# A hand-ordered decoder layer: ScalarE's weight split moved between join and taps, VectorE's adds a chunk later

## The chip, the core and the metric

The kernel runs on one core of one Trainium2 chip. The metric is the device time of one execution in microseconds; less is better. The engines are TensorE (PE, with PEld for its weight loads), VectorE (DVE), ScalarE (ACT), GpSimd (POOL) and SyncE (SP), which issues most DMAs. Each engine takes its instructions in the order in which the program issues them.

## The reference

One decoder layer in float32, for 256 tokens of width 2048:

```
h    = rms_norm(x, g1);  proj = h @ w_in            # q, k, v, p
a    = attention(norm(q), norm(k), v, rel_bias)     # 8 heads of 128, causal
m    = multiscale_pool(p, pool_w, pool_scale)
x    = x + concat(a, m) @ w_out
u    = rms_norm(x, g2) @ w_up                       # 2 * 5632 columns
y    = conv_b + sum_i conv_w[i] * u[t - 2 + i]      # causal, width 3, per column
gate, val = split(y)
x    = x + (silu(gate) * val) @ w_down
```

The last four lines, the gated feed-forward with the convolution between, are where the change lies.

## The kernel before

**Precision.** Each float32 operand of a product is split in a high part (rounded by a ScalarE copy to the matmul type) and a low part (VectorE: operand minus high part). A product is high x high + high x low + low x high. Weights arrive by DMA as raw tiles and are split on the fly: `high(c)` is the ScalarE copy (wh, L182), `low(c)` the VectorE subtraction (wl, L188).

**Rows, chunks and steps.** The weights lie in HBM as a list of rows (chunks) of 128 x 2048 numbers, in the order of use. A chunk of kind "feat" or "tok" has two steps, one of kind "sum" or "rest" a single one. The loop at the end of `layer` goes over the steps. At the first step of chunk r it issues `high(r+3)` on ScalarE, then `low(r+2)` on VectorE, then the weights' sums (`make`) that are set for r+2, then what the agenda holds for this step, then the list `deferred`, and then the matmuls. `later(2, f)` puts f in the agenda two steps after the first step of the current chunk, for feat chunks the start of the next chunk.

**Feed-forward in thirds.** The 22 groups of 256 gate and 256 value columns are done in thirds of 8, 8 and 6 groups. First come the up blocks of a third, for each group g a gate block and a value block, of two feat chunks each (called R0, R1 for the gate and R2, R3 for the value block here). Then comes the down stage of the third, in two halves, in which the pairs of `SEVEN` use a seven-product scheme in place of eight: it needs sums of weight quarters (`make`, VectorE L196 to L198, written to HBM from its raw tile and loaded again as a "sum" chunk) and sums of activation quarters (`left_sums`, L860 to L865). `BY_DVE` says at which groups of each third the weights' sums are made.

**After each up block** its post function runs, at the end of the block's second chunk:
- `conv_in`, the join: ScalarE copies one half of the PSUM result (fs, L545), VectorE adds the other half (L546) and multiplies with the row factor into u (L801).
- `conv`, the taps: six ScalarE instructions form the three products of the convolution from u (y, L811, and z, L813).
- `rest`, through `deferred` at the start of the next chunk: `taps`, two VectorE adds (L819; called the adds here), then Silu on ScalarE for a gate block (L832), or VectorE's product with the gate (L845) and ScalarE's high part of hid (L846) for a value block.
- `rest2`, a chunk after a value block's rest: hid's low part (L850) and, where the pair is one of seven products, `left_sums`, with ScalarE's high part (L864). Its low part (L865) waits in the list `pending` until the next gate block's post function.

**Buffers.** raw tiles: five; wh: four; wl: three; PSUM results of up blocks: two; the scratch tiles of fs and z: two together; u: one for gate and one for value blocks; the buffer of left sums (ls) is shared with the gate's y (tag y0).

Of the kernel before, what the change touches and what calls it, by code (L numbers as in the profile page):

```python
# [23 lines left out]
F32 = mybir.dt.float32  # L24
F32R = mybir.dt.float32r
AF = mybir.ActivationFunctionType
OP = mybir.AluOpType
AX = mybir.AxisListType

P = 128  # L30
D = 2048
S = 256
# [5 lines left out]
NF = DFF // P  # L38
# [17 lines left out]
STAGES = (0, 2, 4, 6)  # L56
EARLY = (72, 72, 80, 80)
BY_DMA = ((), (), ())
BY_DVE = ((2, 3, 4, 5, 6, 7), (0, 0.5, 1, 2, 3, 4, 5, 6, 6.5, 7), (0, 1, 2, 3, 4, 5))
SOFF, SPAD = 32, 64  # L60


# [6 lines left out]
def plan():  # L69

    rows = [(k, i) for i, k in enumerate(24 * ["tok"] + 25 * ["feat"])]
    makes, t = [(u, None) for u in EARLY], 0
    for (g0, g1), sevens, by_dma, by_dve in zip(THIRDS, SEVEN, BY_DMA, BY_DVE):
        c = rows[-1][1] + 1
        makes += [(2 * c + u, None) for u in by_dma] + [(None, len(rows) + int(4 * p) + 3) for p in by_dve]
        rows += [("feat", c + i) for i in range(4 * (g1 - g0))]
        c = rows[-1][1] + 1
        for i in range(2 * (g1 - g0)):
            if i % (g1 - g0) in sevens:
                rows.append(("sum", t))  # L80
                t += 1
            rows.append(("rest" if i % (g1 - g0) in sevens else "tok", c + i))
    assert len(makes) == t, (len(makes), t)
    return rows, makes
# [12 lines left out]
def layer(ctx: ExitStack, tc: tile.TileContext, xT, wts, mix, mix12, par, rel_d, ident_d, icnt_d, out):  # L97
    nc = tc.nc
# [15 lines left out]
    def small(name):  # L114
        return sm.tile([P, 512], F32, name=name, tag="small")
# [3 lines left out]
    def col(c):  # L119
        return pv[:, c:c + 1]  # L120
# [3 lines left out]
    rows, makes = plan()  # L124
# [6 lines left out]
    late, turn_of = {}, [0]  # L131
# [93 lines left out]
    def load_next():  # L225

        if order:
            c = order.pop(0)
            if not isinstance(c, tuple) and c < KT // 2:
                load_xT(2 * c, 2 * c + 2)  # L230
            load(c)
# [94 lines left out]
    ps = small("ps_start")  # L326
# [91 lines left out]
    rrow = keep.tile([P, S], F32, name="rrow", tag="rrow")  # L418
# [124 lines left out]
    def add_halves(dst, ps):  # L543

        nc.scalar.activation(dst, ps[:, :, S:], AF.Copy)  # L545
        nc.vector.tensor_tensor(dst, ps[:, :, :S], dst, op=OP.add)  # L546
# [52 lines left out]


    steps, hooks, pre, deferred = [], [], {}, []
    hold, splits, now, agenda, pending = set(), [], [0], {}, []
    where = []

    def later(n, f):
        agenda.setdefault(now[0] + n, []).append(f)
# [12 lines left out]
    def feat_block(act, ks, post, final=False):  # L619
        box, runs = {}, []  # L620
        for i, k0 in enumerate(ks):
            def run(u, i=i, k0=k0):
                if i == 0:
                    box["acc"] = None if final else acc("ps_feat")
                    box["ps"] = [small("ps_feat")[:, :S] if final else box["acc"][:, m, :] for m in range(2)]
                feat_half(u, act(), k0, box["ps"], i == 0, i == len(ks) - 1, feat_sum if final else feat_mm)
                if i == len(ks) - 1:
                    post(box["ps"] if final else box["acc"])
            runs.append([run])
        return runs  # L630
# [46 lines left out]
    for b in range(2):  # L677
# [6 lines left out]
        for j in range(4):  # L684
            h = 4 * b + j
            u, ul, uo = ((32, 35, 40), (40, 44, 48), (48, 52, 55), (55, 59, 63))[h // 2]
# [8 lines left out]
    def open_late():  # L695
        ectx.close()
        pool = ctx.enter_context(tc.tile_pool(name="late", bufs=1))
        late["pool"] = pool
        late["x2f"] = [block("x2f").rearrange("p (k t) -> p k t", t=S) for _ in range(4)]
        for k0, k1 in ((0, 2), (2, 4), (4, 8), (8, 12), (12, KT)):  # L700
            nc.sync.dma_start(x2_tiles(k0, k1), xT[:, KT + k0 * S:KT + k1 * S].rearrange("p (k t) -> p k t", t=S))
        late["sq"] = pool.tile([P, 2, S], F32, name="sq2", tag="y1")
        late["u"] = [pool.tile([P, 2, 2 + S], F32, name=f"u{i}") for i in range(2)]
        for u in late["u"]:
            nc.gpsimd.memset(u[:, :, :2], 0.0)
        load_next()

    def x2_tiles(k0, k1):
        return late["x2f"][k0 // 4][:, k0 % 4:k0 % 4 + k1 - k0, :]

    def scratch(name):
        return late["pool"].tile([P, 2, S], F32, name=name, tag="fs", bufs=2)

    def block(name, dt=F32):
        return late["pool"].tile([P, SPAD + 1024], dt, name=name, tag="sums", bufs=5)[:, SOFF:SOFF + 1024]
# [55 lines left out]
    def stats2():  # L771
        late["rrow"] = keep.tile([P, S], F32, name="rrow2", tag="rrow")
        a, b = scratch("rs0"), scratch("rs1")
        t = a[:, 0, :]
        mean_sq(t.rearrange("p (j a) -> p a j", a=32), late["row"].rearrange("p (a j) -> p a j", j=8))
        rsqrt(late["rrow"], t, S, late["pool"], (a[:, 1, :], b[:, 0, :]))
# [16 lines left out]
    after(o0 + 4, open_late)  # L793


    def conv_in(ps, which):

        u = late["u"][which]
        s = scratch("fs")
        add_halves(s, ps)  # L800
        nc.vector.tensor_tensor(u[:, :, 2:], s, late["rrow"][:, None, :].to_broadcast([P, 2, S]), op=OP.mult)  # L801

    def conv(f0_, which):

        u = late["u"][which]
        y = late["pool"].tile([P, 2, S], F32, name="y", tag=f"y{which}")
        z = [scratch("z") for _ in range(2)]
        for m in range(2):
            f = f0_ + m
            cw = [col(C_CW + i * 2 * NF + f) for i in range(3)]  # L810
            nc.scalar.activation(y[:, m, :], u[:, m, 2:], AF.Identity, scale=cw[2], bias=col(C_CB + f))  # L811
            for i in range(2):
                nc.scalar.activation(z[i][:, m, :], u[:, m, 1 - i:1 - i + S], AF.Copy, scale=cw[1 - i])  # L813
        return y, z

    def taps(y, z):

        for t in z:
            nc.vector.tensor_tensor(y, y, t, op=OP.add)  # L819
        return y  # L820

    def gate(ps, g):
        if g == 0:
            stats2()
        while pending:
            pending.pop()()
        conv_in(ps, 0)
        parts = conv(2 * g, 0)

        def rest():  # L830
            y = taps(*parts)
            nc.scalar.activation(y, y, AF.Silu)  # L832
            late["gate"] = y
        deferred.append(rest)

    def value(ps, g, j, seven):
        conv_in(ps, 1)
        parts = conv(NF + 2 * g, 1)

        def rest():  # L840
            if j == 0:
                late["hid"] = keep.tile([P, KT, 2, S], F32R, name="hid", tag="c")
            y = taps(*parts)
            hid, ks = late["hid"], slice(2 * j, 2 * j + 2)
            nc.vector.tensor_tensor(y, y, late["gate"], op=OP.mult)  # L845
            nc.scalar.activation(hid[:, ks, 0, :], y, AF.Copy)  # L846
            later(2, lambda: rest2(y, hid, ks))

        def rest2(y, hid, ks):
            nc.vector.tensor_tensor(hid[:, ks, 1, :], y, hid[:, ks, 0, :].bitcast(F32), op=OP.subtract)  # L850
            if seven:
                late["S", j] = left_sums(y)
        deferred.append(rest)

    def left_sums(y):

        y = y.rearrange("p a (b n) -> p (a b) n", n=P)
        a11, a21, a12 = (y[:, i, :] for i in range(3))
        s = late["pool"].tile([P, 2, S], F32, name="ls", tag="y0").rearrange("p a (b n) -> p (a b) n", n=P)
        nc.vector.tensor_tensor(s[:, :2, :], y[:, 0:4:3, :], y[:, 1:2, :].to_broadcast([P, 2, P]), op=OP.subtract)  # L860
        nc.vector.tensor_tensor(s[:, 2, :], s[:, 1, :], a11, op=OP.add)
        nc.vector.tensor_tensor(s[:, 3, :], a12, s[:, 2, :], op=OP.subtract)
        parts = block("sums", F32R).rearrange("p (a b n) -> p a b n", a=2, n=P)
        nc.scalar.activation(parts[:, 0], s, AF.Copy)  # L864
        pending.append(lambda: nc.vector.tensor_tensor(parts[:, 1], s, parts[:, 0].bitcast(F32), op=OP.subtract))  # L865
        return parts

    def product(ps, left, right, first, last):
# [68 lines left out]
    for n, ((g0, g1), sevens) in enumerate(zip(THIRDS, SEVEN)):  # L937
        ups = []
        for g in range(g0, g1):
            ups.append(feat_block(lambda: late["h"], XK, lambda ps, g=g: gate(ps, g)))  # L940
            ups.append(feat_block(lambda: late["h"], XK,
                                  lambda ps, g=g, j=g - g0, sevens=sevens: value(ps, g, j, j in sevens)))
        u0 = len(steps)
        steps += [h for b in ups for h in b]
        if n == 0:
# [46 lines left out]
    n = len(steps)  # L992
# [43 lines left out]
def chunks(w_in, pool_w, w_out, w_up, w_down):  # L1036

    def tok(w, c0):
        return [w[k:k + 256, c0:c0 + 512].reshape(2, P, 512).transpose(1, 0, 2).reshape(P, HALF)
                for k in range(0, D, 256)]  # L1040

    (_, makes), mix, mix12 = plan(), [], []

    def pair(w, k, c0, seven):
# [65 lines left out]
```

## Time and profile before

| | |
|---|---|
| median of 3 runs | 997.92 us (997.23 to 999.34) |
| profiled execution, device time | 999.23 us |
| its span, first to last instruction | 997.5 us |
| TensorE busy | 988.4 us (99%) |
| VectorE busy | 824.1 us (83%) |
| ScalarE busy | 612.8 us (61%) |
| GpSimd busy | 74.8 us (7%) |
| mean granted TensorE clock | 0.998 |

In the profile a line such as "L188 DVE TENSOR_TENSOR wl<-raw,wh" is an instruction by its line in the kernel, its engine, its operation, and its output and inputs by their names in the program. A timeline row gives the start in us from the span's start, the duration (of all merged ones, with their count as x2), and in brackets how long the engine was idle before and what ended that. Neighbouring instructions of an engine overlap by some hundredths of a microsecond, so the distance from start to start is the better price of one. A TensorE busy share of 99% is that of a pipelined engine whose ends are modelled.

### The profile page before, as it was taken

To read this page: it belongs to the slowest core of one execution; us is meant where nothing else is said; L and a number is where in the kernel's file an instruction comes from. 1 tells how busy PE (TensorE), PEld (TensorE's weight loads), DVE (VectorE), ACT (ScalarE), POOL (GpSimd) and SP (SyncE) were. 2 spreads that over 40 slices of the span, in tenths; PEclk is the share of its full clock that TensorE was granted. 3 is DMA by queue.
4 is the path that set the end of the run, shared out by engine and by line. 5 is a ranking of instruction groups with operands and counts; after the bars stand their busy time and mean duration, and the time that the engine had idled before them with its cause. 6 is when DMAs were issued, how large, how long until landed. Compare 5 with 4: busy or idle time off the path is not lost.

```text
span 997.5 us, 13509 instructions
## 1 busy us (share of the span) xinstructions
PE 988.4 (99%) x5276; PEld 853.3 (86%) x5276; DVE 824.1 (83%) x853; ACT 612.8 (61%) x719; POOL 74.8 (7%) x135
## 2 busy tenths in 40 slices
PE   9999999999999999999999999999999999999998
PEld 8888888898888888888888888888878888888886
DVE  6776858867678988889888888888988878888986
ACT  6554546456447777677755666677685646777752
POOL 0302232211113300000000000000000000000000
PEclk9999999999999999999999999999999999999999
DMA  9959685699978887777977797777897958777882
GB/s 345 320 205 296 232 260 198 208 322 373 316 199 290 309 302 280 283 276 267 388 291 305 290 366 294 265 274 296 318 347 278 390 210 332 275 274 264 300 315 90
DMA packets 48895, 285.34 MB, mean 286 GB/s; under 512 B 6696, under 2 KB 9128, under 8 KB 20352
## 3 DMA queue, kind: packets, MB, share of 16 engines
q1 hardware_dynamic: 41776, 264.17, 71.8%
q0 software_dynamic: 7056, 20.33, 7.8%
q8 instruction: 41, 0.67, 0.3%
q14 instruction: 22, 0.18, 0.1%
HBM read 253.14 MB, written 39.72 MB: 294 GB/s over the span
## 4 chain that ended last, share of the span: by engine, by line
PE 66%; ACT 12%; DVE 11%; issue 6%; DMA 3%; POOL 1%; ACTq 0%; POOLq 0%; DVEq 0%
PE ps_feat L276 26%; PE ps_down L871 20%; PE ps_feat L278 13%; ACT wh L182 5%; PE ps_val L254 4%; ACT z L813 3%; ACT y L811 2%; PE ps_tok L264 2%; DVE wl L188 2%; DVE u L801 2%; DVE fs L546 1%; DVE raw L196 1%; DMA qT<-q1d 1%; DVE raw L197 1%; DVE raw L198 1%
## 5 line engine op out<-in xcount | busy, mean ns | idle before, releaser
L276 PE MATMUL ps_feat<-x2h,wh 128*128 128x512 f32 x1406 | 479.2, 389 | 0.0
L188 DVE TENSOR_TENSOR wl<-raw,wh 128x2048 fp32r<-128x2048 f32 (+1 forms) x171 | 376.2, 2207 | 35.8 <-ACT wh L182 19.9
L278 PE MATMUL ps_feat<-x2h,wl 128*128 128x256 f32 x1408 | 389.1, 276 | 0.7 <-DVE wl L188 0.6
L182 ACT ACTIVATE wh<-raw 128x2048 fp32r<-128x2048 f32 (+1 forms) x171 | 315.4, 1849 | 86.8 <-PE ps_down L871 60.3
L276 PEld LDWEIGHTS ps_feat<-x2h,wh 128*128 128x128 f32 x1406 | 263.9, 188 | 55.2
L278 PEld LDWEIGHTS ps_feat<-x2h,wl 128*128 128x128 f32 x1408 | 264.3, 188 | 1.3 <-DVE wl L188 1.3
L871 PE MATMUL ps_down<-wh,hid 128*128 128x512 f32 x444 | 142.7, 390 | 0.0
L160 DVE TENSOR_TENSOR wl<-raw,wh 128x2048 fp32r<-128x2048 f32 (+3 forms) x44 | 83.0, 1895 | 38.0 <-ACT wh L159 29.4
L811 ACT ACTIVATE y<-u,pv 128x256 f32<-128x256 f32 x88 | 52.4, 595 | 78.4 <-DVE u L801 78.4
L871 PEld LDWEIGHTS ps_down<-wh,hid 128*128 128x128 f32 x444 | 83.6, 188 | 17.4
L276 PE MATMUL ps_feat<-cat,wh 128*128 128x512 f32 x256 | 87.3, 389 | 0.0
L871 PE MATMUL ps_down<-wl,hid 128*128 128x512 f32 x222 | 86.6, 390 | 0.1
L264 PE MATMUL ps_tok<-wh,xh 128*128 128x512 f32 x256 | 80.1, 391 | 0.0
L813 ACT ACTIVATE z<-u,pv 128x256 f32<-128x256 f32 x176 | 78.8, 495 | 0.0
L159 ACT ACTIVATE wh<-raw 128x2048 fp32r<-128x2048 f32 (+3 forms) x44 | 69.4, 1598 | 10.7 <-DMA raw<-in_wts 7.5
L819 DVE TENSOR_TENSOR y<-y,z 128x512 f32<-128x512 f32 x88 | 60.9, 693 | 14.7 <-ACT z L813 9.4
L871 PE MATMUL ps_down<-wh,sums 128*128 128x512 f32 x208 | 70.6, 395 | 0.4 <-ACT wh L182 0.4
L278 PE MATMUL ps_feat<-cat,wl 128*128 128x256 f32 x256 | 70.7, 276 | 0.0
L546 DVE TENSOR_TENSOR fs<-ps_feat,fs 128x512 f32<-128x512 f32 x52 | 35.8, 689 | 39.9 <-ACT fs L545 39.6
L264 PEld LDWEIGHTS ps_tok<-wh,xh 128*128 128x128 f32 x256 | 48.1, 188 | 10.0
L276 PEld LDWEIGHTS ps_feat<-cat,wh 128*128 128x128 f32 x256 | 48.1, 188 | 9.8
L545 ACT ACTIVATE fs<-ps_feat 128x512 f32<-128x512 f32 x52 | 30.4, 585 | 39.6 <-PE ps_feat L278 38.2
(189 smaller groups left out, 1015.9 us busy)
## 6 DMA issues: line engine op xcount, KB each, us to landing
raw<-in_wts SPq DMA_DIRECT2D x152, 1024.0 KB, 6.8
raw<-mixed SPq DMA_DIRECT2D x26, 1024.0 KB, 6.5
raw<-in_mix SPq DMA_DIRECT2D x22, 1024.0 KB, 4.9
mixed<-raw SPq DMA_DIRECT2D x22, 1024.0 KB, 5.0
raw<-in_wts SPq DMA_DIRECT2D x26, 768.0 KB, 5.0
raw<-in_wts SPq DMA_DIRECT2D x4, 512.0 KB, 7.3
mixed<-in_mix POOLq DMA_DIRECT2D x4, 512.0 KB, 14.5
mixed<-mixed POOLq DMA_DIRECT2D x8, 256.0 KB, 8.6
```

The source lines that it names most:

```text
L159: nc.scalar.activation(wh, w, AF.Copy)
L160: nc.vector.tensor_tensor(wl, w, wh.bitcast(F32), op=OP.subtract)
L182: nc.scalar.activation(w, raws[c][:, :width(c)], AF.Copy)
L188: nc.vector.tensor_tensor(wl, raws[c][:, :width(c)], wh.bitcast(F32), op=OP.subtract)
L264: nc.tensor.matmul(ps[:, t, :], act[:, k0 + k, a, ts], w[:, ws], start=(first and k == 0 and n == 0), stop=(last and k == 1 and n == 2))
L276: nc.tensor.matmul(ps, wh[:, ws], act[:, k, :, :], start=(bool(first) and n == 0), stop=False, skip_group_check=True)
L278: nc.tensor.matmul(ps[:, S:], wl[:, ws], act[:, k, 0, :], start=False, stop=(last and n == len(ks) - 1), skip_group_check=True)
L546: nc.vector.tensor_tensor(dst, ps[:, :, :S], dst, op=OP.add)
L811: nc.scalar.activation(y[:, m, :], u[:, m, 2:], AF.Identity, scale=cw[2], bias=col(C_CB + f))
L813: nc.scalar.activation(z[i][:, m, :], u[:, m, 1 - i:1 - i + S], AF.Copy, scale=cw[1 - i])
L819: nc.vector.tensor_tensor(y, y, t, op=OP.add)
L871: nc.tensor.matmul(ps, a, w, start=(first and n == 0), stop=(last and n == 2), skip_group_check=True)
```

## The change

- ScalarE: the taps of a block are not issued in its post function any more but through `deferred` at the start of the next chunk. So `high` of that chunk (and what the agenda has) comes between the join's copy and the taps.
- VectorE: the adds and what follows them (`rest`) come one chunk later than before, through `later(2, ...)`; only the last value block of a third keeps them right behind its taps (`end`).
- Left sums: the low part comes through `later(2, ...)` a chunk after the high part, not in the next gate block's post function; the list `pending` goes. The buffer ls gets a tag of its own.
- u: one buffer for gate and value blocks instead of two.
- Weights' sums: those of a whole number in `BY_DVE` are made in the first chunk of the group's gate block (R0) instead of the second (R1); those of a half number stay in R3. In third 1 the one at 6.5 goes to 1.5, in third 2 the one at 5 goes to 0.5.

```diff
--- before.py
+++ after.py
@@ -56,7 +56,7 @@
 STAGES = (0, 2, 4, 6)
 EARLY = (72, 72, 80, 80)
 BY_DMA = ((), (), ())
-BY_DVE = ((2, 3, 4, 5, 6, 7), (0, 0.5, 1, 2, 3, 4, 5, 6, 6.5, 7), (0, 1, 2, 3, 4, 5))
+BY_DVE = ((2, 3, 4, 5, 6, 7), (0, 0.5, 1, 1.5, 2, 3, 4, 5, 6, 7), (0, 0.5, 1, 2, 3, 4))
 SOFF, SPAD = 32, 64
 
 
@@ -72,7 +72,7 @@
     makes, t = [(u, None) for u in EARLY], 0
     for (g0, g1), sevens, by_dma, by_dve in zip(THIRDS, SEVEN, BY_DMA, BY_DVE):
         c = rows[-1][1] + 1
-        makes += [(2 * c + u, None) for u in by_dma] + [(None, len(rows) + int(4 * p) + 3) for p in by_dve]
+        makes += [(2 * c + u, None) for u in by_dma] + [(None, len(rows) + 4 * int(p) + (5 if p % 1 else 2)) for p in by_dve]
         rows += [("feat", c + i) for i in range(4 * (g1 - g0))]
         c = rows[-1][1] + 1
         for i in range(2 * (g1 - g0)):
@@ -599,7 +599,7 @@
 
 
     steps, hooks, pre, deferred = [], [], {}, []
-    hold, splits, now, agenda, pending = set(), [], [0], {}, []
+    hold, splits, now, agenda = set(), [], [0], {}
     where = []
 
     def later(n, f):
@@ -700,9 +700,8 @@
         for k0, k1 in ((0, 2), (2, 4), (4, 8), (8, 12), (12, KT)):
             nc.sync.dma_start(x2_tiles(k0, k1), xT[:, KT + k0 * S:KT + k1 * S].rearrange("p (k t) -> p k t", t=S))
         late["sq"] = pool.tile([P, 2, S], F32, name="sq2", tag="y1")
-        late["u"] = [pool.tile([P, 2, 2 + S], F32, name=f"u{i}") for i in range(2)]
-        for u in late["u"]:
-            nc.gpsimd.memset(u[:, :, :2], 0.0)
+        late["u"] = pool.tile([P, 2, 2 + S], F32, name="u")
+        nc.gpsimd.memset(late["u"][:, :, :2], 0.0)
         load_next()
 
     def x2_tiles(k0, k1):
@@ -793,16 +792,15 @@
     after(o0 + 4, open_late)
 
 
-    def conv_in(ps, which):
-
-        u = late["u"][which]
+    def conv_in(ps):
+
         s = scratch("fs")
         add_halves(s, ps)
-        nc.vector.tensor_tensor(u[:, :, 2:], s, late["rrow"][:, None, :].to_broadcast([P, 2, S]), op=OP.mult)
+        nc.vector.tensor_tensor(late["u"][:, :, 2:], s, late["rrow"][:, None, :].to_broadcast([P, 2, S]), op=OP.mult)
 
     def conv(f0_, which):
 
-        u = late["u"][which]
+        u = late["u"]
         y = late["pool"].tile([P, 2, S], F32, name="y", tag=f"y{which}")
         z = [scratch("z") for _ in range(2)]
         for m in range(2):
@@ -822,22 +820,22 @@
     def gate(ps, g):
         if g == 0:
             stats2()
-        while pending:
-            pending.pop()()
-        conv_in(ps, 0)
-        parts = conv(2 * g, 0)
-
-        def rest():
+        conv_in(ps)
+
+        def rest(parts):
             y = taps(*parts)
             nc.scalar.activation(y, y, AF.Silu)
             late["gate"] = y
-        deferred.append(rest)
-
-    def value(ps, g, j, seven):
-        conv_in(ps, 1)
-        parts = conv(NF + 2 * g, 1)
-
-        def rest():
+
+        def start():
+            parts = conv(2 * g, 0)
+            later(2, lambda: rest(parts))
+        deferred.append(start)
+
+    def value(ps, g, j, seven, end):
+        conv_in(ps)
+
+        def rest(parts):
             if j == 0:
                 late["hid"] = keep.tile([P, KT, 2, S], F32R, name="hid", tag="c")
             y = taps(*parts)
@@ -846,23 +844,30 @@
             nc.scalar.activation(hid[:, ks, 0, :], y, AF.Copy)
             later(2, lambda: rest2(y, hid, ks))
 
+        def start():
+            parts = conv(NF + 2 * g, 1)
+            if end:
+                rest(parts)
+            else:
+                later(2, lambda: rest(parts))
+        deferred.append(start)
+
         def rest2(y, hid, ks):
             nc.vector.tensor_tensor(hid[:, ks, 1, :], y, hid[:, ks, 0, :].bitcast(F32), op=OP.subtract)
             if seven:
                 late["S", j] = left_sums(y)
-        deferred.append(rest)
 
     def left_sums(y):
 
         y = y.rearrange("p a (b n) -> p (a b) n", n=P)
         a11, a21, a12 = (y[:, i, :] for i in range(3))
-        s = late["pool"].tile([P, 2, S], F32, name="ls", tag="y0").rearrange("p a (b n) -> p (a b) n", n=P)
+        s = late["pool"].tile([P, 2, S], F32, name="ls", tag="ls").rearrange("p a (b n) -> p (a b) n", n=P)
         nc.vector.tensor_tensor(s[:, :2, :], y[:, 0:4:3, :], y[:, 1:2, :].to_broadcast([P, 2, P]), op=OP.subtract)
         nc.vector.tensor_tensor(s[:, 2, :], s[:, 1, :], a11, op=OP.add)
         nc.vector.tensor_tensor(s[:, 3, :], a12, s[:, 2, :], op=OP.subtract)
         parts = block("sums", F32R).rearrange("p (a b n) -> p a b n", a=2, n=P)
         nc.scalar.activation(parts[:, 0], s, AF.Copy)
-        pending.append(lambda: nc.vector.tensor_tensor(parts[:, 1], s, parts[:, 0].bitcast(F32), op=OP.subtract))
+        later(2, lambda: nc.vector.tensor_tensor(parts[:, 1], s, parts[:, 0].bitcast(F32), op=OP.subtract))
         return parts
 
     def product(ps, left, right, first, last):
@@ -939,7 +944,7 @@
         for g in range(g0, g1):
             ups.append(feat_block(lambda: late["h"], XK, lambda ps, g=g: gate(ps, g)))
             ups.append(feat_block(lambda: late["h"], XK,
-                                  lambda ps, g=g, j=g - g0, sevens=sevens: value(ps, g, j, j in sevens)))
+                                  lambda ps, g=g, j=g - g0, sevens=sevens, end=g == g1 - 1: value(ps, g, j, j in sevens, end)))
         u0 = len(steps)
         steps += [h for b in ups for h in b]
         if n == 0:
```

## The prediction

> **What bounds the kernel now.** I read the page first, then busy time by stretch, then the timelines of TensorE, ScalarE and VectorE. The page gives the span and each engine's busy time and share.
>
> ```profile
> span 997.5 us, 13509 instructions
> ...
> PE 988.4 (99%) x5276; PEld 853.3 (86%) x5276; DVE 824.1 (83%) x853; ACT 612.8 (61%) x719; POOL 74.8 (7%) x135
> ```
>
> TensorE is the bound, so the change can only act through stalls of TensorE or its clock. The feed-forward part has three thirds, each with feat blocks (w_up) and then a down stage (w_down). Busy time by stretch: first number the length, then TensorE, its weight loads, VectorE, ScalarE, GpSimd, the granted clock, the DMA share and GB/s.
>
> ```profile
> 285.30:461.40 176.10, 175.43 (x1026) 154.32 (x1025) 153.55 (x165) 119.61 (x163) 20.78 (x38) 1.00 0.78 275
> 461.40:474.00 12.60, 12.40 (x56) 9.95 (x55) 11.53 (x10) 10.98 (x15) 0.00 (x0) 1.00 0.87 299
> 542.20:716.30 174.10, 174.10 (x1026) 154.02 (x1025) 152.90 (x155) 113.00 (x152) 0.00 (x0) 1.00 0.80 298
> 716.30:734.00 17.70, 15.35 (x59) 11.78 (x58) 15.77 (x14) 14.86 (x18) 0.00 (x0) 0.90 0.86 292
> 801.50:932.00 130.50, 130.50 (x770) 115.81 (x769) 110.88 (x110) 85.85 (x115) 0.00 (x0) 1.00 0.75 275
> ```
>
> The rows from 285.30, 542.20 and 801.50 are the feat blocks of thirds 0, 1 and 2: 16, 16 and 12 blocks. Third 1 takes 174.10 / 16 = 10.88 us a block, and third 2 the same (130.50 / 12), with TensorE busy throughout. Third 0 takes 176.10, so 2.0 us are lost; 0.2 idle follow in its transition to down. The transition of third 1, from 716.30, has 2.35 us idle and a clock of 0.90: 10% of 17.7 us, another 1.8 us. There TensorE stands still twice:
>
> ```profile
> 726.70 0.39 PE L871 MATMUL ps_down<-wh,sums 128*128 128x512 f32 x1
> 727.52 0.49 PE L871 MATMUL ps_down<-wh,sums 128*128 128x512 f32 x1 [0.43 <-ACT wh L182]
> 729.85 0.50 PE L871 MATMUL ps_down<-wl,sums 128*128 128x512 f32 x1 [1.83 <-DVE wl L188]
> ```
>
> Against the 0.23 us from one matmul to the next of an undisturbed stream (174.10 us hold 513 pairs of a 512- and a 256-column matmul, 0.339 us a pair), 726.70 to 727.52 loses 0.59 us and 727.52 to 729.85 loses 2.10 us. The second wait names VectorE's low part wl (L188). All that can be won is thus 2.0 + 0.2 + 2.7 + 1.8 = 6.7 us.
>
> Why VectorE is late there shows in one group of third 1 (a gate and a value block, one weights' sum, left sums). ScalarE first:
>
> ```profile
> 667.56 0.58 ACT L545 ACTIVATE fs<-ps_feat 128x512 f32<-128x512 f32 x1
> 669.80 0.60 ACT L811 ACTIVATE y<-u,pv 128x256 f32<-128x256 f32 x1 [1.66 <-DVE u L801]
> 670.31 0.89 ACT L813 ACTIVATE z<-u,pv 128x256 f32<-128x256 f32 x2
> 671.11 0.59 ACT L811 ACTIVATE y<-u,pv 128x256 f32<-128x256 f32 x1
> 671.60 0.90 ACT L813 ACTIVATE z<-u,pv 128x256 f32<-128x256 f32 x2
> 672.40 1.91 ACT L182 ACTIVATE wh<-raw 128x2048 fp32r<-128x2048 f32 x1
> 674.22 0.62 ACT L832 ACTIVATE y<-y 128x512 f32<-128x512 f32 x1
> 674.73 1.91 ACT L182 ACTIVATE wh<-raw 128x2048 fp32r<-128x2048 f32 x1
> 676.54 0.57 ACT L545 ACTIVATE fs<-ps_feat 128x512 f32<-128x512 f32 x1
> ...
> 683.25 0.63 ACT L846 ACTIVATE hid<-y 128x512 fp32r<-128x512 f32 x1
> ...
> 689.65 0.63 ACT L864 ACTIVATE sums<-ls 128x512 fp32r<-128x512 f32 x1 [3.96 <-DVE ls L862]
> 690.19 0.58 ACT L545 ACTIVATE fs<-ps_feat 128x512 f32<-128x512 f32 x1
> ```
>
> VectorE in the same group:
>
> ```profile
> 677.15 0.69 DVE L546 TENSOR_TENSOR fs<-ps_feat,fs 128x512 f32<-128x512 f32 x1 [0.51 <-ACT fs L545]
> 677.88 0.69 DVE L801 TENSOR_TENSOR u<-fs,rrow 128x512 f32<-128x512 f32 x1
> 678.49 2.29 DVE L188 TENSOR_TENSOR wl<-raw,wh 128x2048 fp32r<-128x2048 f32 x1
> 680.94 1.49 DVE L819 TENSOR_TENSOR y<-y,z 128x512 f32<-128x512 f32 x2 [0.17 <-ACT z L813]
> 682.46 0.69 DVE L845 TENSOR_TENSOR y<-y 128x512 f32<-128x512 f32 x1
> 683.15 2.29 DVE L188 TENSOR_TENSOR wl<-raw,wh 128x2048 fp32r<-128x2048 f32 x1
> 685.36 1.22 DVE L196 TENSOR_TENSOR raw<-raw 128x1024 f32<-128x1024 f32 x1
> ...
> 687.34 0.69 DVE L198 TENSOR_TENSOR raw<-raw 128x512 f32<-128x512 f32 x1
> 687.95 0.69 DVE L850 TENSOR_TENSOR hid<-y,hid 128x512 fp32r<-128x512 f32 x1
> 688.55 0.42 DVE L860 TENSOR_TENSOR ls<-y 128x256 f32<-128x256 f32 x1
> ...
> 689.33 0.29 DVE L862 TENSOR_TENSOR ls<-y,ls 128x128 f32<-128x128 f32 x1
> ```
>
> From one gate join's copy fs (667.56) to the next (690.19) pass 22.63 us, while TensorE needs 2 x 10.88 = 21.76. The two engines hand work to and fro and fall 0.87 us behind in each such group, though VectorE was busy for only 152.90 of 174.10 us. The lateness of the join copies, first and last of a third:
>
> ```profile
> 320.43 0.58 ACT L545 ACTIVATE fs<-ps_feat 128x512 f32<-128x512 f32 x1
> ...
> 463.29 0.57 ACT L545 ACTIVATE fs<-ps_feat 128x512 f32<-128x512 f32 x1
> ...
> 553.30 0.60 ACT L545 ACTIVATE fs<-ps_feat 128x512 f32<-128x512 f32 x1 [3.61 <-PE ps_feat L278]
> ...
> 720.91 0.57 ACT L545 ACTIVATE fs<-ps_feat 128x512 f32<-128x512 f32 x1
> ```
>
> In third 1 the first copy is 553.30 - 542.2 - 10.88 = 0.2 us after its block, the last 720.91 - 716.3 = 4.6. In third 0 the last is 463.29 - (285.3 + 174.1) = 3.9 late, the copy of group 1's gate block (320.43, third of its blocks) 2.5. Third 2 loses nothing.
>
> **The change, part by part.** The operations and their count stay: only order, places and two buffers change. So the cost is a new period of the same chain, which I build from start-to-start distances of the rows above.
>
> *From a gate join to the value join* (chunks R2 and R3 of a group). VectorE: add 0, u at 0.73 (677.15 to 677.88), low 1.34 (678.49), then hid's low part after 2.21 (683.15 to 685.36) at 3.55, left sums at 4.15 (687.95 to 688.55), their last at 4.93, and ScalarE's copy of them 0.32 after it (689.33 to 689.65) at 5.25. This copy comes from the agenda, so it stands ahead of the deferred taps of ScalarE (conv). They start 0.54 later (689.65 to 690.19) at 5.79 and last 2.60 (669.80 to 672.40): 8.39. Then comes R3's high part, 1.82 (672.40 to 674.22): 10.21. VectorE has meanwhile done R3's low part, the sums' low part and the adds, and Silu runs 0.51 (674.22 to 674.73). Only then comes the value join's copy: 10.72, and its add 0.61 later (676.54 to 677.15): 11.33.
>
> *From the value join to the next gate join* (R0 and R1). VectorE: add 0, u 0.73, low 1.34, weights' sum 3.55 to 6.14 (three instructions, 685.36 to 687.95 is 2.59), R1's low part to 8.35, two adds of 0.76 each (680.94 to 682.46 is 1.52) 9.87, and the gate product, on which ScalarE's hid copy follows 0.79 later (682.46 to 683.25): 10.66. The gate join's copy stands behind it: 0.54 more, 11.20, and its add 11.81.
>
> Together 23.14 us, about 0.1 less where adds follow closer; I take 23.05. The high part now runs while VectorE joins, and that does remove ScalarE's wait of 1.66 us before y (669.80). But the adds, one chunk later, put Silu and the hid copy directly ahead of the next join's copy, in ScalarE's order. VectorE therefore idles before both joins. Each group with a weights' sum and left sums falls back 23.05 - 21.76 = 1.29 us instead of 0.87.
>
> *Third 1.* Weights' sums now lie in groups 0 and 1 twice and in every other group once, and one of 6.5 is gone. From group 0's gate copy (0.2 late) to group 7's are seven periods: 0.2 + 7 x 1.29 = 9.2 late, taking the first two, with a second sum but no left sums, like the others. The last half group has no left sums: add 0, u 0.73, low 1.34, hid's low part 3.55, low 4.15, adds 6.36, Silu about 7.9, copy 8.4, add 9.0 instead of 10.88, so 1.9 come back: 7.3 late against 4.6, 2.7 more. At the end the last rest is not delayed, but a high part of 1.82 lies between the join's copy and the taps. Now the taps start 2.06 after the copy (the same from 676.54 to 678.60); then 0.58 + 1.82 = 2.40: 0.34 more until this low part, which frees TensorE:
>
> ```profile
> 727.50 2.29 DVE L188 TENSOR_TENSOR wl<-raw,wh 128x2048 fp32r<-128x2048 f32 x1
> ```
>
> So TensorE stands 3.0 us longer in third 1. Its clock loss of 1.8 is there already.
>
> *Third 0.* Six sums from group 2 on. 2.5 late at group 1's gate, about as much at group 2's (no sum between), five periods of 1.29 more: 9.0, less 1.9: 7.1 against 3.9. With the 0.34 this is 3.5 us longer. Its end stall grows from a fraction of a microsecond, at clock 1.00 (row from 461.40), to over 3 us, longer than what cost third 1 its clock, so I add the same 1.8 us; its bounds are 0 and 1.8.
>
> *Third 2.* Three groups with left sums and no sum in the last group. Lateness stays under 5 us (0.2 and at most three or four periods of 1.29), and third 1 bears more today: the copy at 690.19 is 6.6 us after its block (the 13th: 542.2 + 141.4), with TensorE busy throughout. So 0 here; a lateness 1 us above that cover would cost 1 us.
>
> *DMAs and queues.* A weights' sum for a whole p is one chunk earlier; its load, its store and the load after it on SP move with it, none is added.
>
> ```profile
> raw<-in_wts SPq DMA_DIRECT2D x152, 1024.0 KB, 6.8
> ...
> mixed<-raw SPq DMA_DIRECT2D x22, 1024.0 KB, 5.0
> ```
>
> A load behind such a store lands 5.0 + 6.8 = 11.8 us after the sum, two chunks of 5.44, and a load is asked for about four chunks ahead. So I take 0; if sums in neighbouring chunks (0.5 and 1, 1.5 and 2) make a raw tile late, high waits and now the taps behind it: up to 1 us each, in third 1 alone, 2 to 4 us as the upper bound. *One u instead of two:* the taps have read it by 8.39 and the value join writes it at 11.33 + 0.73 = 12.06, so 3.7 us of cover; if that goes, u waits up to one set of taps, 2.60. *Own buffer for left sums, no pending list, one memset fewer on GpSimd:* VectorE does the same 0.69 us in R3, in the shade of ScalarE's taps; 0.
>
> **The sum.** 3.0 + 3.5 + 1.8 = 8.3 us on the profiled execution's 999.23 us: 1007.5. The median of the runs shown, 997.92, lies 1.3 lower, so 1006.2. On the clock the Trainium skill, "TensorE: Matmul & The Clock Gate", Part 1, has a rule: the clock halves after at least one idle window of about 3.4 us. The row from 716.30, 0.90 after stops of 0.6 and 2.1 us, does not agree; by that rule an end stall of some 3 us in third 0 would cost no clock, and the sum would be 1004.4.
>
> **The rivals.**
> *Faster: the chain drops under 21.76.* If the join's copy is not held by Silu and the hid copy, because their adds are long done, VectorE's own work sets the pace: 152.90 / 8 = 19.1 us a group. All stalls go: 997.92 - 6.7 = 991.2. For it speaks that ScalarE's wait for u (1.66) vanishes. It needs 1.3 us off my period; against it, the adds come behind VectorE's low parts and sums and end just before the join is due. It decides once the period is under 21.76. 0.09.
> *No change:* the period stays at 22.6, waits only change places: 997.9. It needs my period 0.4 too long. 0.06.
> *Slower, and late weights besides:* the upper bound above, 2 to 4 us more: about 1009. The landing times speak against a steady loss. 0.15.
> *Slower, as summed:* 0.70.
>
> **How the numbers follow.** The forecast is 1006.2 us. 0.4 us less on the period over seven and five groups takes 2.8 and 2.0 us off, to 1001.4; late weights put 1010 at the top. The range 1001 to 1010 leaves out the faster and the unchanged case and some of the tails. Slower by over 0.2% (2 us, about what a measurement can tell from no change): 0.85; within: 0.06; faster: 0.09.
>
> **What the changed profile would show.** Right: ScalarE's order copy, high, taps; VectorE's main waits at the join's add, on ScalarE's fs, with Silu or hid just before it; gate copies some 23.0 us apart in thirds 0 and 1; the last copies 7 us late; TensorE waiting 0.3 to 0.8 us for wl in the later groups and over 3 us at both transitions, with a clock under 1.00 at both. Wrong: copies 21.8 us apart and no waits of TensorE, or ScalarE's high waiting for raw.

## The result and the profile after

| | before | after |
|---|---|---|
| median | 998.63 us (4 runs) | 1009.68 us (4 runs, 1007.6 to 1011.52) |
| profiled execution | 999.23 us | 1010.49 us |
| gate copies apart in a full group | 22.63 us | 23.09 us |

The changed kernel takes 1.011 times as long, with a 95% interval of 1.0084 to 1.0137: 11 us more, where 1006.2 with a range of 1001 to 1010 was forecast: inside the range, but 0.3 us under its upper end. The page after:

```profile
span 1008.7 us, 13494 instructions
...
PE 993.8 (99%) x5276; PEld 854.3 (85%) x5276; DVE 818.8 (81%) x853; ACT 608.6 (60%) x719; POOL 74.6 (7%) x134
```

The work is the same and the span 11.2 us longer; VectorE and ScalarE have a smaller share than before. The stretches that answer to those of before: feat blocks of third 0, its transition, the same of third 1, feat blocks of third 2 (length, then busy times from TensorE on, clock, DMA share, GB/s):

```profile
284.70:462.00 177.30, 175.87 (x1026) 154.13 (x1025) 149.46 (x162) 116.88 (x160) 20.78 (x38) 1.00 0.77 274
462.00:481.00 19.00, 15.80 (x61) 12.05 (x60) 16.64 (x16) 13.61 (x19) 0.00 (x0) 0.91 0.72 244
547.90:725.20 177.30, 176.60 (x1026) 154.40 (x1025) 150.00 (x154) 112.73 (x152) 0.00 (x0) 1.00 0.79 299
725.20:747.00 21.80, 18.26 (x67) 13.95 (x66) 18.63 (x16) 15.65 (x20) 0.00 (x0) 0.84 0.66 235
812.70:943.30 130.60, 130.60 (x770) 115.90 (x769) 110.82 (x110) 85.27 (x114) 0.00 (x0) 1.00 0.76 285
```

The feat blocks of thirds 0 and 1 take 177.30 us each, 3.2 more than an undisturbed 174.1. TensorE is idle for 19.00 - 15.80 = 3.2 us in the first transition and 21.80 - 18.26 = 3.5 us in the second, and the clock there is 0.91 and 0.84. Third 2 loses nothing. All waits of TensorE for a low part of the weights:

```profile
PE ps_down L876 <- DVE wl L188: 6.7, 4, 3.0
PE ps_feat L278 <- DVE wl L188: 1.7, 5, 0.6
```

One full group, ScalarE and then VectorE (start, duration, instruction, in brackets the idle time before it and what ended it):

```profile
652.68 0.58 ACT L545 ACTIVATE fs<-ps_feat 128x512 f32<-128x512 f32 x1
...
658.54 0.63 ACT L869 ACTIVATE sums<-ls 128x512 fp32r<-128x512 f32 x1 [3.46 <-DVE ls L867]
...
661.66 1.91 ACT L182 ACTIVATE wh<-raw 128x2048 fp32r<-128x2048 f32 x1
663.48 0.61 ACT L827 ACTIVATE y<-y 128x512 f32<-128x512 f32 x1
663.99 0.58 ACT L545 ACTIVATE fs<-ps_feat 128x512 f32<-128x512 f32 x1
664.47 1.91 ACT L182 ACTIVATE wh<-raw 128x2048 fp32r<-128x2048 f32 x1
...
675.23 0.63 ACT L844 ACTIVATE hid<-y 128x512 fp32r<-128x512 f32 x1 [4.46 <-DVE y L843]
675.77 0.58 ACT L545 ACTIVATE fs<-ps_feat 128x512 f32<-128x512 f32 x1
```

```profile
661.39 1.49 DVE L817 TENSOR_TENSOR y<-y,z 128x512 f32<-128x512 f32 x2
664.60 0.69 DVE L546 TENSOR_TENSOR fs<-ps_feat,fs 128x512 f32<-128x512 f32 x1 [1.72 <-ACT fs L545]
...
672.93 1.48 DVE L817 TENSOR_TENSOR y<-y,z 128x512 f32<-128x512 f32 x2
674.44 0.69 DVE L843 TENSOR_TENSOR y<-y 128x512 f32<-128x512 f32 x1
676.38 0.69 DVE L546 TENSOR_TENSOR fs<-ps_feat,fs 128x512 f32<-128x512 f32 x1 [1.24 <-ACT fs L545]
```

Read the two side by side. The taps of the gate block are over at 661.66, and the next high part runs to 663.48. VectorE has done its adds (661.39 and on) and stands idle for 1.72 us. What it waits for, the value join's copy fs (663.99), is third on ScalarE, behind high and Silu (663.48). In the second half ScalarE is idle for 4.46 us before hid's copy (675.23), since VectorE makes the gate product only at 674.44; the gate join's copy (675.77) stands behind it, and VectorE then waits 1.24 us for that copy. Without hid's copy ahead of it, it could have gone some 2 us earlier, when the first add (half of the two from 672.93) has read z and so freed one of the two scratch tiles that fs and z share; this is an estimate from the rows, and e2 below shows that wait. From 652.68 to 675.77 are 23.09 us. Before the change ScalarE waited for VectorE's u; that wait is gone, and VectorE waits for ScalarE's copy instead:

```profile
L546 DVE TENSOR_TENSOR fs<-ps_feat,fs 128x512 f32<-128x512 f32 x52 | 36.0, 692 | 83.8 <-ACT fs L545 83.8
```

83.8 us idle before the join's add in the whole run, all of it for fs; before the change VectorE waited 39.6 us for fs there.

### The profile page after: what moved, and what is told of

It is laid out like the page before. It is cut to its first block, busy times and chain, and to the rows that moved or that the text cites. A ratio compares the mean times of both kernels' runs of the same rounds, so it can differ in the third digit from the quotient of the medians.

```text
span 1008.7 us, 13494 instructions
## 1 busy us (share of the span) xinstructions
PE 993.8 (99%) x5276; PEld 854.3 (85%) x5276; DVE 818.8 (81%) x853; ACT 608.6 (60%) x719; POOL 74.6 (7%) x134
## 4 chain that ended last, share of the span: by engine, by line
PE 61%; DVE 19%; issue 7%; ACT 7%; DMA 5%; POOL 1%; SPq 0%; DVEq 0%; ACTq 0%; POOLq 0%
PE ps_feat L276 22%; PE ps_down L876 20%; PE ps_feat L278 11%; DVE wl L188 8%; PE ps_val L254 4%; DVE y L817 2%; DVE fs L546 2%; ACT z L811 2%; PE ps_tok L264 2%; ACT fs L545 1%; ACT wh L182 1%; ACT y L809 1%; DVE raw L196 1%; DVE u L799 1%; DMA qT<-q1d 1%
## 5 line engine op out<-in xcount | busy, mean ns | idle before, releaser
L546 DVE TENSOR_TENSOR fs<-ps_feat,fs 128x512 f32<-128x512 f32 x52 | 36.0, 692 | 83.8 <-ACT fs L545 83.8
L844 ACT ACTIVATE hid<-y 128x512 fp32r<-128x512 f32 x22 | 13.9, 633 | 81.8 <-DVE y L843 81.8
```

## The experiments

Theory: in ScalarE's order Silu and hid's copy, which now come a chunk later, stand directly ahead of the next join's copy, and the join and all behind it wait. Rival 1: it is high ahead of the taps. Rival 2: it is the places of the weights' sums. The kernels were run in three groups, each beside the kernel before, whose medians were then 997.96 (e1 to e4), 998.88 (e5 to e8) and 999.11 us (e9 and e10); each ratio is against its own group's.

**e1: the adds at once.**

```diff
             parts = conv(2 * g, 0)
-            later(2, lambda: rest(parts))
+            rest(parts)
...                                   # and the same in value's start
```

> The change with one part undone: the adds (and Silu, the gate product, hid's copy) follow right behind their taps again, as before the change; high stays ahead of the taps, the weights' sums and buffers stay as changed. Theory (Silu and hid's copy, moved a chunk later, stand ahead of the next join's copy in ScalarE's order): the distance of gate copies in a group with a weights' sum and left sums falls from 23.08 to 21.8 us, TensorE never waits in thirds 0 and 1, and the 19.5 us lost in the feed-forward part go: about 990 to 992 us. Rival 1 (high ahead of the taps delays the taps, and VectorE waits for them): the distance stays near 23, about 1009. Rival 2 (two weights' sums in neighbouring chunks crowd VectorE): stays too, above 1004.

Measured: 992.65 us, ratio 0.9949 (0.9932 to 0.9966). ScalarE in a full group of third 1:

```profile
666.59 0.58 ACT L545 ACTIVATE fs<-ps_feat 128x512 f32<-128x512 f32 x1
667.06 1.92 ACT L182 ACTIVATE wh<-raw 128x2048 fp32r<-128x2048 f32 x1
668.87 0.59 ACT L809 ACTIVATE y<-u,pv 128x256 f32<-128x256 f32 x1
...
672.85 0.63 ACT L827 ACTIVATE y<-y 128x512 f32<-128x512 f32 x1 [1.30 <-DVE y L817]
673.39 1.92 ACT L182 ACTIVATE wh<-raw 128x2048 fp32r<-128x2048 f32 x1
675.21 0.58 ACT L545 ACTIVATE fs<-ps_feat 128x512 f32<-128x512 f32 x1
...
688.52 0.58 ACT L545 ACTIVATE fs<-ps_feat 128x512 f32<-128x512 f32 x1
```

Copy, high (667.06), taps (668.87), Silu (672.85), another high and only then the next copy (675.21): Silu has a chunk's high part between itself and the copy. The gate copies lie 688.52 - 666.59 = 21.93 us apart, 0.1 more than expected. TensorE waits once for a low part:

```profile
PE ps_down L873 <- DVE wl L188: 0.3, 1, 0.3
```

The time lies 0.65 us above the range that was expected. So the whole loss hangs on the adds' chunk, and without that move the rest of the change gains. Both rivals fall as causes of the loss.

**e2: Silu and hid's copy behind the next join's copy**, the adds still a chunk later.

```diff
         s = scratch("fs")
-        add_halves(s, ps)
+        nc.scalar.activation(s, ps[:, :, S:], AF.Copy)
+        while behind:
+            behind.pop(0)()
+        nc.vector.tensor_tensor(s, ps[:, :, :S], s, op=OP.add)
...
-            nc.scalar.activation(y, y, AF.Silu)
+            behind.append(lambda: nc.scalar.activation(y, y, AF.Silu))
...
+            copy = lambda: nc.scalar.activation(hid[:, ks, 0, :], y, AF.Copy)
+            copy() if end else behind.append(copy)
```

> The change whole, the adds a chunk later included, but Silu and hid's copy are issued just behind the next join's copy on ScalarE instead of ahead of it. Theory: the join's copy no longer waits for adds, the distance of gate copies is 21.8 us, about 990 to 992 us. Rival 1 (high ahead of the taps) and rival 2 (places of the weights' sums) change nothing here: near 1009. A third reading (the adds being late is itself the cost, because hid and the left sums are late for the down stage) gives 1009 or more.

Measured: 992.04 us, ratio 0.9942 (0.9927 to 0.9957). Third 1, feat blocks and transition:

```profile
539.80:713.90 174.10, 174.10 (x1026) 154.53 (x1025) 154.68 (x158) 116.41 (x156) 0.00 (x0) 1.00 0.82 311
713.90:731.00 17.10, 17.10 (x78) 14.17 (x77) 14.71 (x13) 14.12 (x15) 0.00 (x0) 1.00 0.66 235
```

TensorE is busy throughout, at full clock; gate copies are 662.35 - 641.12 = 21.23 us apart, faster than TensorE's 21.76, since the chain is catching up:

```profile
641.12 0.60 ACT L798 ACTIVATE fs<-ps_feat 128x512 f32<-128x512 f32 x1 [2.41 <-DVE y L820]
...
662.35 0.60 ACT L798 ACTIVATE fs<-ps_feat 128x512 f32<-128x512 f32 x1 [2.40 <-DVE y L820]
```

Late adds as such cost nothing that these times show. It is the place of two ScalarE instructions of 0.6 us each against a third. One part of the theory did not hold: the gate join's copy still waits for adds, 2.4 us for the first of them (L820), since fs takes a scratch tile that z held. What it no longer waits for is the second add, the gate product and hid's copy.

**e5 and e6: one of the two alone.** The diffs are the lines of e2 for Silu and for hid's copy.

> The change whole, with Silu alone issued behind the value join's copy; hid's copy stays ahead of the gate join's copy. Theory: the first half of the chain (gate join to value join) loses its wait of 1.7 us on VectorE, the second half keeps its 1.2; the distance of gate copies in a full group is 22.4 to 22.6 us instead of 23.08, and 1 to 3 us stay lost: 992 to 995 us. If Silu were not in the way: 1009.

> The change whole, with hid's copy alone issued behind the gate join's copy; Silu stays ahead of the value join's copy. Theory: the gate join no longer waits for the gate product, which lies behind the weights' sum; the chain is cut there, the distance is 21.8 us and nearly nothing stays lost: 991 to 993 us. If hid's copy were not in the way: 1009; if each of the two gave half: about 1000.

e6: 992.34 us, ratio 0.9932 (0.9917 to 0.9946), gate copies 662.53 - 640.77 = 21.76 apart: moving hid's copy alone gives all of it.

```profile
640.77 0.60 ACT L798 ACTIVATE fs<-ps_feat 128x512 f32<-128x512 f32 x1 [2.92 <-DVE y L820]
...
662.53 0.60 ACT L798 ACTIVATE fs<-ps_feat 128x512 f32<-128x512 f32 x1 [2.93 <-DVE y L820]
```

e5: 999.05 us, ratio 1.0003 (0.9993 to 1.0014), where 992 to 995 was expected. So moving Silu alone takes away the loss against the kernel before, but gains nothing. The distance itself came out as expected, 22.56 in a full group: VectorE's wait in the first half shrank from 1.72 to 1.20 us, as R3's high part still runs ahead of the copy, and did not go as the theory had it. But 22.56 is still over 21.76, and between the gate copies of groups 1 and 2 of third 1 it was 25.19:

```profile
574.74 0.58 ACT L798 ACTIVATE fs<-ps_feat 128x512 f32<-128x512 f32 x1
578.90 1.93 ACT L182 ACTIVATE wh<-raw 128x2048 fp32r<-128x2048 f32 x1 [3.59 <-DMA raw<-in_wts]
...
588.16 0.57 ACT L798 ACTIVATE fs<-ps_feat 128x512 f32<-128x512 f32 x1
...
599.93 0.58 ACT L798 ACTIVATE fs<-ps_feat 128x512 f32<-128x512 f32 x1
```

574.74 to 588.16 is the first half of group 1, 13.42 us. High waits 3.59 us for its weights, and VectorE then 1.30 us for high (until 580.87) and 0.64 us for the weights of the sum (until 583.80).

**e10 and e9: third 1's sum at 1.5 moved to 3.5**, in e5 and in the changed kernel.

```diff
-(0, 0.5, 1, 1.5, 2, 3, 4, 5, 6, 7)
+(0, 0.5, 1, 2, 3, 3.5, 4, 5, 6, 7)
```

> As the run with Silu alone behind the join's copy (999.05 us), but the sum at 1.5 of third 1 lies at 3.5, so that groups 0 and 1 don't have four of them in neighbouring chunks. There, two gate copies followed after 25.2 us instead of 22.56, and high waited up to 3.6 us for weights. Reading a (late weights from the crowding make that jump): the waits go, 1 to 2 us less late at the end of the third, 996 to 998 us. Reading b (a second sum simply adds its 2.6 us to a chain that never catches up, wherever it lies): the same lateness, 999 us.

> The changed kernel with the sum at 1.5 of third 1 at 3.5, nothing else. Reading a: group 1's distance falls from 23.4 to 21 to 22 us, but the second sum lengthens group 3 by less than 1 us as the ScalarE half of the chain covers it: 1007 to 1009 us. Reading b: 1009.7 us.

e10: 998.28 us, ratio 0.9991 (0.9979 to 1.0003). ScalarE's waits for weights in the feat blocks of third 1 and its transition fell from 16.9 to 6.6 us, and the last copy of the third was 4.1 us late instead of 5.7. So late weights were part of the lateness, but the time lies between the two readings, and e10 and e5 can't be told apart with these intervals. e9: 1009.67 us, ratio 1.0099 (1.0072 to 1.0127). ScalarE's waits for weights in the same stretch fell from 5.6 to 2.6 us, and the last copy was 8.3 late instead of 9.0; the time is that of the changed kernel, as reading b said. Group 1's distance fell to 20.8 us, but group 3's rose by 1.9 to 25.0, not by less than 1. So undoing this part of the crowding takes 0.7 us off the 9.0 of lateness, and nothing off the time that these intervals show.

**e3: the change with the sums at their old places.**

> The change with the weights' sums at the places from before the change (second chunk of the gate block, and 6.5 and 5 in place of 1.5 and 0.5). Theory: the period of 23.1 us does not hang on where in the group the sum lies; thirds 0 and 1 stay, third 2 has a sum in its last group again and loses 1 to 3 us: 1009 to 1013 us. Rival 2 (the new places are the cost): back towards 998.

Measured: 1013.79 us, ratio 1.017 (1.0139 to 1.0201), 0.8 above what was expected. Third 2, which loses nothing in the changed kernel, now does: its feat blocks (12 x 10.88 = 130.6) and its transition:

```profile
808.80:940.00 131.20, 131.20 (x773) 116.01 (x773) 107.83 (x108) 84.14 (x114) 0.00 (x0) 1.00 0.72 272
940.00:966.00 26.00, 23.01 (x95) 18.44 (x94) 22.98 (x17) 19.21 (x18) 0.00 (x0) 0.93 0.84 305
```

0.6 us in the blocks, 3.0 idle in the transition, and a clock of 0.93. The new places help; rival 2 has the sign wrong.

**e4: the kernel before with the new places alone.**

> The kernel before with nothing but the new places of the weights' sums. Theory: in the old order the sum in the second chunk stood on VectorE ahead of hid's low part and the left sums, on which ScalarE waited 4.0 us a group; in the first chunk it does not, so the period falls from 22.63 to about 22.2 and, with the last groups of a third freed, the stalls of the feed-forward part (7.7 us) go: 991 to 994 us. Rival 2: slower than before, above 1000.

Measured: 993.29 us, ratio 0.9956 (0.9938 to 0.9973). Gate copies (642.85 and 665.14) are 22.29 apart.

**e8: high ahead of the taps, adds at once, sums at their old places.**

> High ahead of the taps, adds at once behind the taps, weights' sums at their old places, buffers and left sums' low part as in the change. Theory: high ahead of the taps is no cost, the distance is 22.3 to 22.5 us against 22.63 before, about 1 us stays lost in third 1: 992 to 994 us. Rival 1 (high ahead of the taps delays them): 998 or above.

Measured: 994.67 us, ratio 0.9953 (0.9938 to 0.9969), 0.7 above the range that was expected, gate copies (663.93 and 686.32) 22.39 apart. High ahead of the taps, taken together with the left sums' low part a chunk later and the two buffers, is a gain, so rival 1 has the sign wrong as well. The buffers alone make little of it (e7); high and the low part were not run apart.

**e7: the two buffers alone, in the kernel before** (one u; the tag ls for the left sums).

> The kernel before with one u for gate and value blocks and a buffer of its own for the left sums, nothing else. Theory: no one waits for either, 998 us, distance 22.63. A reading in which the single u or the shared buffer matters: 1 us or more away from that.

Measured: 997.43 us over 10 runs, ratio 0.9988 (0.9978 to 0.9999): gate copies 22.57 apart, about a tenth of a percent gained, by the interval 0.01 to 0.22%.

The best versions, e1, e2, e4 and e6, lie between 992.0 and 993.3 us with overlapping intervals; the kernel before lies 0.4 to 0.7% above them. They can't be told from each other; in each of them TensorE waits for weights of the feed-forward part for under 1 us.

## Why the prediction was right, point by point

*The mechanism.* The period was worked out as 23.05 us and is 23.09; both idle times of VectorE stand where they were forecast, with Silu and hid's copy ahead of the copy, and e1, e2 and e6 show that the loss hangs on that order. Third 2 lost nothing, as said: its copies were at most 4.7 us late, though four periods, which the prediction allowed, would have made 5.4 and not "under 5". Fewer waits for loads did not make the changed kernel faster by anything that could be measured (e9).

*The sum.* 8.3 us were forecast and 11.1 came. By the rows after against those of before: third 0 loses 1.2 us more in its blocks and 3.0 more in its transition, 4.2 where 3.5 stood; its clock 1.7 (9% of 19.00) where 1.8 stood. Third 1 loses 3.2 more in its blocks and 1.2 (3.5 against 2.35) in its transition, 4.4 where 3.0 stood, and its clock 3.5 (16% of 21.80) against 1.8, 1.7 more where 0 stood. These are 12.0 us; 0.6 come back since the feed-forward part began that much earlier in this execution, which leaves 11.4 against 11.3 between the two profiled executions. The measured time came near the top of the range, 1010, which was set there for late weights; other terms filled it. So the range held in part by luck.

*The terms that were too small.* First, "taking the first two, with a second sum but no left sums, like the others". The first copies of third 1:

```profile
559.02 0.60 ACT L545 ACTIVATE fs<-ps_feat 128x512 f32<-128x512 f32 x1 [3.63 <-PE ps_feat L278]
...
564.79 1.92 ACT L182 ACTIVATE wh<-raw 128x2048 fp32r<-128x2048 f32 x1 [0.78 <-DMA raw<-in_wts]
570.82 0.63 ACT L827 ACTIVATE y<-y 128x512 f32<-128x512 f32 x1 [4.11 <-DVE y L817]
571.36 0.58 ACT L545 ACTIVATE fs<-ps_feat 128x512 f32<-128x512 f32 x1
```

From gate copy to value copy of group 0 pass 12.34 us, where a full group's half takes 11.3: the sum at 0.5 lies in this half. The 0.78 us that high waited for its weights held up nothing, as Silu waited 4.11 us for VectorE after it; VectorE itself stood idle for 1.25 us before R3's low part (564.51). The first two periods are 24.12 and 23.38 us, so they make 4.0 us of lateness where two of 1.29 stood; why VectorE was idle there was not tested. The last copy

```profile
730.95 0.58 ACT L545 ACTIVATE fs<-ps_feat 128x512 f32<-128x512 f32 x1
```

is 730.95 - 547.9 - 174.1 = 9.0 us late, not 7.3. In third 0 the lateness was likewise 8.6 at the end and not 7.1: the gate copies of groups 1 and 2 were already 3.7 (321.02 - 284.7 - 32.64) and 3.8 late where 2.5 stood for both. The runs do not show why. Second, "Its clock loss of 1.8 is there already": the loss grew. Which transition it grew in was chance, as e9 shows below; the two together lose 5.2 us by the clock, in e9 5.0, where 3.6 stood.

*The clock.* The Trainium skill's rule ("TensorE: Matmul & The Clock Gate", Part 1), an idle window of about 3.4 us that runs freely, gives 1004.4 if read as a stop of at least 3.4 us. The longest stop here was 3.0 us by the row of the waits, and the clock fell in both transitions, as the shares of 0.91 and 0.84 show: the trace does not agree with that reading. Less idle time in one window is enough, as the last section works out.

*The rivals.* "Faster" needed the copy free of Silu and hid's copy: this is e2, 992.0 us where that rival's time was 991.2. "Late weights besides": its time, about 1009, is the nearest to what was measured, but by other terms. Such waits exist in third 1 (5.6 us in its feat blocks, the longest 2.0, more than the 1 us given), and the prediction counted ScalarE's high waiting for raw among the signs of being wrong; but with more than half of these waits gone the time stayed (e9).

## What to carry to other kernels

When an engine works its queue in order, moving a consumer later puts it ahead of something else: name what now stands behind it, and what that waits for. Here two 0.6 us instructions went ahead of the copy that another engine needed next, one of them after a wait of 4.46 us for that same engine, and a loop of the two engines grew from 22.6 to 23.1 us against TensorE's 21.8. Price such an order as a period, start to start around the loop, against the bound's period, and add up the lateness until the buffers' cover is gone; put work that waits behind work that others wait for.

## What the runs showed of the hardware

*The clock.* The length of a stop of TensorE alone does not tell whether its clock falls, nor for how long. Before the change stops of 0.6 and 2.1 us in one transition went with a clock of 0.90. In e5 a longer one, 2.8 us, left it whole; its waits for low parts, and its transition of third 1 (3.3 us idle, clock 1.00):

```profile
PE ps_down L879 <- DVE wl L188: 4.5, 3, 2.8
```

```profile
714.80:734.00 19.20, 15.90 (x72) 12.69 (x71) 17.25 (x15) 15.74 (x22) 0.00 (x0) 1.00 0.65 227
```

In the changed kernel the two transitions lose 1.7 us (third 0) and 3.5 us (third 1) by the clock. In e9, with all but the same idle time in them, it is the other way round. Its rows for the transition of third 0, the 9 us behind it, and the transition of third 1:

```profile
462.00:481.00 19.00, 15.79 (x64) 12.09 (x63) 16.64 (x15) 14.79 (x21) 0.00 (x0) 0.90 0.71 257
481.00:490.00 9.00, 9.00 (x35) 7.29 (x34) 7.07 (x4) 5.12 (x3) 0.00 (x0) 0.84 0.95 331
725.20:747.00 21.80, 18.22 (x75) 14.09 (x74) 19.40 (x18) 16.69 (x22) 0.00 (x0) 0.92 0.66 232
```

Third 0 loses 10% of 19.00 and 16% of 9.00, together 3.3 us, and third 1 8% of 21.80, 1.7 us. What decides is how a stop lies on a fixed grid. In the traces every stretch at half clock between the first 15 us and the last matmul lasts 3.41 or 6.83 us, and all of them begin a whole number of 3.413 us after the trace's first record of the clock, whatever the kernel does then. Cut on that grid, the transition of third 1 reads like this, in the changed kernel and then in e5:

```profile
735.72:739.13 3.41, 1.35 (x6) 0.75 (x4) 3.27 (x4) 1.47 (x3) 0.00 (x0) 1.00 0.77 296
739.13:742.54 3.41, 2.52 (x6) 2.04 (x7) 3.41 (x4) 3.41 (x3) 0.00 (x0) 0.50 0.45 123
742.54:745.95 3.41, 3.41 (x9) 2.64 (x9) 3.10 (x2) 1.33 (x2) 0.00 (x0) 0.50 0.99 358
```

```profile
725.21:728.62 3.41, 2.33 (x11) 1.59 (x9) 2.60 (x4) 1.47 (x4) 0.00 (x0) 1.00 0.93 308
728.62:732.03 3.41, 1.67 (x7) 1.41 (x8) 3.41 (x3) 3.41 (x4) 0.00 (x0) 1.00 0.22 36
```

In the changed kernel TensorE is idle for 2.06 us of one window, and the next two are at half clock; in e5 the same kind of stop is spread as 1.08 and 1.74 us over two, and the clock stays (the window behind them is at 1.00). In this part of all twelve traces, eight windows with 2.0 to 3.0 us idle were each followed by one at half clock, and of twelve with 0.7 to 1.8 us idle one was (1.76 us, in e7). A window at half clock that was itself idle for 0.7 to 0.9 us was followed by another (two cases), one with at most 0.5 us was not. The grid lies differently against the kernel's start in each trace, so which stop is hit is chance. A window at half clock in which TensorE is busy throughout costs 1.7 us.

Between the fastest and the slowest run of the changed kernel lie 3.9 us. The mean clock of the four runs goes with it: 0.997 in the two faster ones, 0.995 and 0.994 in the others. Of 1008 us these are 3 us lost against 5 to 6, so the clock accounts for 2 to 3 of the 3.9 us, by this estimate.

*A slower pace at full clock.* Not all of the 3.2 us that third 1's feat blocks lose are stops. From 645.82 to 656.70 TensorE ran 66 matmuls, and from 667.58 to 678.46, after first short waits, 64, busy throughout and at a clock of 1.00 in both; pairs of matmuls then start 0.35 us apart and not 0.34. Added up over the third this is about 1.3 us, by the distances of the starts. The runs do not show why.
